# Branch merges, held modulation rounds and up products of a two-block kernel on one core

## The chip, the core and the metric

The kernel runs on one core of a Trainium2 chip. Times are device microseconds (us) of one execution. Engines: PE is TensorE (matrix products), PEld its weight load, DVE VectorE, ACT ScalarE, POOL GpSimd (here it mostly issues DMAs), SP the queue that issues the weight loads.

## The reference, cut to what is computed

256 tokens of width 1024 pass through two blocks of two layers each. All is fp32. The first block is attention with a dense feed-forward layer, then attention with a mixture of experts (MoE). The change touches the second block most:

```python
def merge_branches(y_ml, y_ga, y_na, zg, w_branch, w_out):
    gates = jax.nn.sigmoid(zg).reshape(B, T, N_BRANCH, D_MODEL)
    ys = jnp.stack([y_ml, y_ga, y_na], axis=2)
    proj = jnp.einsum('btnc,ncd->btnd', ys, w_branch)
    return jnp.sum(gates * proj, axis=2) @ w_out

def conv_ffn(h, w_up, conv_w, conv_b, w_down):
    u = h @ w_up
    up = jnp.pad(u, ((0, 0), (1, 1), (0, 0)))
    u = up[:, :-2] * conv_w[0] + up[:, 1:-1] * conv_w[1] + up[:, 2:] * conv_w[2] + conv_b
    a, g = jnp.split(u, 2, axis=-1)
    return (a * jax.nn.silu(g)) @ w_down

# second_block, for each layer l; last = (l == 1)
mod = silu(c) @ w_mod[l] + b_mod[l]          # mod_c from c_ctx alike
sh1, sc1, ga1, sh2, sc2, ga2 = split(mod, 6)
h = modulate(rms_norm(x, g_pre_mix[l]), sh1, sc1)      # hc from the context alike
... = split(h @ w_in[l])                     # three branches, and zg: 3 x 1024 gates
o = merge_branches(y_ml, y_ga, y_na, zg, w_branch[l], w_out[l])
x = x + ga1 * rms_norm(o, g_post_mix[l])
f = conv_ffn(modulate(rms_norm(x, g_pre_ffn[l]), sh2, sc2), w_up[l], conv_w[l], conv_b[l], w_down[l])
x = x + ga2 * rms_norm(f, g_post_ffn[l])
# the 256 context tokens take the same path, in layer 0 only
```

## The kernel before

**Products.** Every fp32 product is three passes in fp32r: the activations and the weights are each cut into a high and a low part, and h·h, h·l and l·h are summed in PSUM. A raw weight tile of 128x1024 (512 KB) comes in from SP's queue, ACT casts it to `wh` (L300) and DVE subtracts to `wl` (L301). Raw tiles stand in a ring of four, `wh` and `wl` in rings of four each. `gemm` (L427, `mac` L421) is **token-major**: a block of 128 tokens stands in the array and 512 weight columns move, so the result lies with tokens on the partitions. `gemm_f` (L472) is **feature-major**: a weight block stands, and the tokens move, 256 for one path or 512 where the context (c) and the image (x) go together; the result lies with features on the partitions. PSUM has three banks "mm" for products, and single banks "tr", "y", "aT", "z0", "z1"; transposes go by a product with the identity (`tr`, L323).

**Order.** A list scheduler lays out every engine's instruction stream ahead of time; it takes the instructions by their order in the program as priority. `side_by_side` (L307) and `bind` (L315) issue a run of products of which all but the first are held behind the one before.

**Modulation.** `mod` (L1031) computes `silu(c) @ w_mod` in rounds: a generator whose every `next` issues loads of `raw<-in_w_mod` on POOL's queue (four of 512 KB for layer 0, two for layer 1) and the round's products `aT<-raw,modS` (eight and four, which the profile counts as 16 and eight), through `side_by_side`. Its 12 rounds for layer 0 are called from the first block's dense feed-forward layer (`block1_dense`, L778): from the loop over the eleven groups of `w_gu` and the one over the two groups of `w_dn`; those for layer 1 from the feed-forward layer of the second block's layer 0. `mod_end` (L1058) evacuates four rounds' sum: part goes to columns, and two of the six kinds to rows in DRAM, which `gag` (L1089) broadcasts to 128 partitions and multiplies with a gain that it broadcasts too (`F<-in_row`).

**MoE.** A first pass takes 128 tokens of each expert; the largest count is read into a register on every engine and a branch goes over the second pass.

**Merge.** In `block2_layer` (L1398), `zgate` computes the gates token-major and stores them to DRAM by POOL (512 KB a path and group). After the attention the loop over the three branches j and the two column groups g loads a gate back (`zgx<-zgx`, L1565, 512 KB, one buffer a path), runs `w_br` token-major, and `mix` multiplies and adds on DVE (L1571, L1574, L1575). Then `u` is transposed (`to_feat`) and split for `w_out`.

**Feed-forward of block 2.** `block2_ffn` (L1615): in layer 1 (image only) group 0 of `w_up` is token-major, evacuated to `tm`, transposed into "tr" (eight transposes) and run through `conv` (one ACT and two DVE instructions for 128 features, L1633, L1634, L1636); groups 1 to 10 are feature-major with 256 moving tokens and run through `conv` straight from the "mm" bank.

## Time and profile before

| | us |
|---|---|
| median of 3 runs | 2661.45 |
| lowest and highest run | 2660.32, 2662.59 |
| the profiled execution's own time | 2667.87 |
| its span in the profile | 2666.1 |

| engine | busy us | share of the span | instructions |
|---|---|---|---|
| PE | 2582.1 | 97% | 13478 |
| DVE | 1778.0 | 67% | 3168 |
| ACT | 1414.4 | 53% | 2180 |
| POOL | 115.9 | 4% | 220 |

Busy time of PE overlaps from one product to the next: a product of 512 columns is listed with about 0.40 us and the next begins 0.23 us after it. So what a stretch costs PE is read from the starts. Idle time in square brackets stands with the instruction that came after it, with the event that ended it. The granted clock is the share of TensorE's full clock that a stretch had; 0.5 is its lower level.

### The profile page before, as it was taken

What the parts mean: (1) busy time and instruction counts of PE and PEld (TensorE: products, weight loads), DVE (VectorE), ACT (ScalarE), POOL (GpSimd) and SP (SyncE); (2) the same over time, 40 slices, a digit from 0 to 9 for tenths busy, and PEclk for the clock granted to TensorE, in tenths of its full rate; (3) what the DMA queues carried; (4) which work ended last, traced back from release to release, by engine and by line L of the source; (5) the groups of instructions that cost most, each with busy time, mean ns of one, the idle gap of its engine ahead of it and who ended that gap; (6) DMA issues with size and microseconds to landing.
All of it is one profiled execution on the core that took longest, in us unless ns stands there. A gap on an engine that the chain in (4) does not pass through costs nothing. (4 is left out here: it accounts for less than half of the span.)

```text
span 2666.1 us, 36388 instructions
## 1 busy us (share of the span) xinstructions
PE 2582.1 (97%) x13478; PEld 2045.5 (77%) x13478; DVE 1778.0 (67%) x3168; ACT 1414.4 (53%) x2180; POOL 115.9 (4%) x220
## 2 busy tenths in 40 slices
PE   8999999999999999899999999999999999998998
PEld 6776776778888888688777787777777787776897
DVE  5865455777888998558665567543546767667785
ACT  6644444565777777444447624432323544664563
POOL 0000110000000000000000000000100000000000
PEclk9999999999999999899999999999999999998999
DMA  6466874454889999442123355444543232455454
GB/s 188 131 194 228 296 269 177 140 177 161 327 319 341 322 332 351 150 141 88 48 64 103 127 182 179 152 165 167 174 142 99 81 127 80 134 195 185 148 184 151
DMA packets 134906, 481.30 MB, mean 181 GB/s; under 512 B 16208, under 2 KB 16368, under 8 KB 134720
## 3 DMA queue, kind: packets, MB, share of 16 engines
q1 hardware_dynamic: 109008, 389.30, 43.0%
q0 software_dynamic: 25424, 89.47, 9.6%
q8 instruction: 109, 1.79, 0.3%
q14 instruction: 77, 0.63, 0.1%
q10 hardware_dynamic: 288, 0.11, 0.0%
HBM read 466.20 MB, written 12.62 MB: 180 GB/s over the span
## 5 line engine op out<-in xcount | busy, mean ns | idle before, releaser
L301 DVE TENSOR_TENSOR wl<-raw,wh 128x1024 fp32r<-128x1024 f32 (+1 forms) x750 | 887.3, 1205 | 245.4 <-ACT wh L300 240.1
L300 ACT CAST wh<-raw 128x1024 fp32r<-128x1024 f32 (+1 forms) x750 | 760.1, 1036 | 334.8 <-PE mm L424 282.9
L423 PE MATMUL mm<-wh,oph 128*128 128x512 f32 (+1 forms) x1248 | 498.9, 401 | 12.1 <-ACT oph L300 7.6
L424 PE MATMUL mm<-wh,opl 128*128 128x512 f32 (+1 forms) x1248 | 496.1, 399 | 4.0 <-DVE opl L301 3.7
L425 PE MATMUL mm<-wl,oph 128*128 128x512 f32 (+1 forms) x1248 | 496.0, 398 | 2.5 <-DVE wl L301 2.3
L488 PE MATMUL mm<-oph,wh 128*128 128x256 f32 (+1 forms) x1024 | 343.1, 337 | 5.4 <-ACT wh L300 2.9
L490 PE MATMUL mm<-oph,wl 128*128 128x256 f32 (+1 forms) x1024 | 341.1, 337 | 0.8 <-DVE wl L301 0.7
L489 PE MATMUL mm<-opl,wh 128*128 128x256 f32 (+1 forms) x1024 | 340.9, 336 | 0.0
L423 PEld LDWEIGHTS mm<-wh,oph 128*128 128x128 f32 x1248 | 237.5, 190 | 80.9 <-ACT oph L300 9.6
L425 PEld LDWEIGHTS mm<-wl,oph 128*128 128x128 f32 x1248 | 237.2, 190 | 68.0 <-issue 12.9
L424 PEld LDWEIGHTS mm<-wh,opl 128*128 128x128 f32 x1248 | 237.8, 191 | 63.8 <-issue 8.8
L488 PEld LDWEIGHTS mm<-oph,wh 128*128 128x128 f32 x1024 | 195.5, 191 | 39.5 <-ACT wh L300 9.3
L490 PEld LDWEIGHTS mm<-oph,wl 128*128 128x128 f32 x1024 | 194.9, 191 | 25.7 <-issue 3.4
L489 PEld LDWEIGHTS mm<-opl,wh 128*128 128x128 f32 x1024 | 195.1, 191 | 20.9 <-issue 1.5
L425 PE MATMUL mm<-wl,moeH 128*128 128x512 f32 (+1 forms) x384 | 146.6, 382 | 0.0
L424 PE MATMUL mm<-wh,moeL 128*128 128x512 f32 (+1 forms) x384 | 145.3, 378 | 0.0
L423 PE MATMUL mm<-wh,moeH 128*128 128x512 f32 (+1 forms) x384 | 145.1, 378 | 0.0
L1633 ACT ACTIVATE F<-mm,cols 128x256 f32<-128x256 f32 (+1 forms) x88 | 57.9, 660 | 102.3 <-PE mm L490 102.1
L423 PE MATMUL mm<-wh,fh 128*128 128x512 f32 x264 | 105.3, 401 | 3.5 <-DVE F L1636 3.5
L1634 DVE SCALAR_TENSOR_TENSOR F<-mm,cols,F 128x255 f32<-128x255 f32 (+1 forms) x88 | 52.8, 602 | 79.9 <-ACT F L1633 78.5
L425 PE MATMUL mm<-wl,fh 128*128 128x512 f32 x264 | 104.9, 399 | 0.0
L424 PE MATMUL mm<-wh,fl 128*128 128x512 f32 x264 | 104.1, 396 | 0.0
(590 smaller groups left out, 3756.3 us busy)
## 6 DMA issues: line engine op xcount, KB each, us to landing
raw<-in_w_in SPq DMA_DIRECT2D x200, 512.0 KB, 4.2
raw<-in_w_gue SPq DMA_DIRECT2D x176, 512.0 KB, 5.5
raw<-in_w_mod POOLq DMA_DIRECT2D x96, 512.0 KB, 7.5
raw<-in_w_up SPq DMA_DIRECT2D x88, 512.0 KB, 4.7
raw<-in_w_dne SPq DMA_DIRECT2D x80, 512.0 KB, 5.0
raw<-in_w_dn SPq DMA_DIRECT2D x66, 512.0 KB, 4.5
raw<-in_w_gu SPq DMA_DIRECT2D x44, 512.0 KB, 4.7
raw<-in_w_out SPq DMA_DIRECT2D x32, 512.0 KB, 3.9
```

Of the source, the lines that this page charges most:

```text
L300: self.nc.scalar.copy(h, src)
L301: self.nc.vector.tensor_tensor(l, src, h.bitcast(F32), op=OP.subtract)
L423: mm(ps, P.h(kc, t), h, start=first, stop=False)
L424: mm(ps, P.l(kc, t), h, start=False, stop=False)
L425: mm(ps, P.h(kc, t), l, start=False, stop=last)
L488: mm(b, hj, xh, start=kc == 0, stop=False)
L489: mm(b, hj, xl, start=False, stop=False)
L490: mm(b, lj, xh, start=False, stop=kc == last)
L1633: nc.scalar.activation(o, s, AF.Identity, scale=cw[1][:, cc:cc + 1], bias=cb[:, cc:cc + 1])
L1634: nc.vector.scalar_tensor_tensor(o[:, :, 1:256], s[:, :, 0:255], cw[0][:, cc:cc + 1], o[:, :, 1:256], op0=OP.mult, op1=OP.add)
```

## The change

- `bind` has a flag `first`, by which the first product of the run is held in program order too; `mod` uses it. In `block1_dense` a round is called in each of the groups of `w_gu` from g = 1 (before: from g = 2), and after `w_dn` 1 + g rounds are called (before: 1 + 2g). There are 12 rounds, as before.
- `mod_end` multiplies the gain into the rows before they are stored; `gag` is one broadcast.
- The register of the MoE's count is read from within the first pass.
- Layer 0: `zgate` and `w_br` are feature-major, 512 tokens moving; gates come back as 128x512 pieces (2 KB in each partition) in a ring of five; `mix` works on features, and its last result is split from SBUF. The transposes of `u` go.
- Layer 1: `w_br` stays token-major; gates come back in the same ring; the transposes of each column group stand behind that group's last branch.
- Layer 1: all eleven groups of `w_up` are token-major, as group 0 was.

```diff
-    def bind(self, run):
+    def bind(self, run, first=False):
...
-            if i:
+            if i or first:
                 self.tc.keep_in_program_order(ins)
...
-                if g > 1:
+                if g:
                     next(mod, None)
...
-                for _ in range(1 + 2 * g):
+                for _ in range(1 + g):
                     next(mod, None)
...
-            self.moe_pass(sp, st, 0)
-            rv = nc.values_load(cnt[0:1, 0:1], min_val=0, max_val=S,
-                                skip_runtime_bounds_check_because="a count of at most 256 tokens")
-            with tc.If(rv > 128):
+            rv = []
+            self.moe_pass(sp, st, 0, lambda: rv.append(nc.values_load(
+                cnt[0:1, 0:1], min_val=0, max_val=S, skip_runtime_bounds_check_because="a count of at most 256 tokens")))
+            with tc.If(rv[0] > 128):
...
-                self.side_by_side(*[p for i in range(0, len(todo), 4) for p in todo[i:i + 4][::-1]])
+                self.bind([lambda p=p: nc.tensor.matmul(*p[:3], skip_group_check=True, **p[3])
+                           for i in range(0, len(todo), 4) for p in todo[i:i + 4][::-1]], first=True)
...
+                    o = ROWS[f"g_om{l}" if kind == 2 else f"g_of{l}"][0] + half * 512
+                    nc.gpsimd.dma_start(gain[p], bass.AP(tensor=src.tensor, offset=src.offset + o, ap=[[0, 2], [1, 512]]))
                     nc.vector.tensor_tensor(bias[p], bias[p], mr[p], op=OP.add)
+                    nc.vector.tensor_tensor(bias[p], bias[p], gain[p], op=OP.mult)
...
-        gp = self.f4.tile([128, D], F32, name="F4", bufs=2)
-        self.rowb(f"g_om{l}" if kind == 2 else f"g_of{l}", gp)
...
-        nc.vector.tensor_tensor(out, out, gp, op=OP.mult)
...
+                def gate(i, t):
+                    gt = sg.tile([128, 512], F32, name="zg", bufs=5)
+                    nc.gpsimd.dma_start(gt, zd[i][:, t])
+                    return gt
...
                     for g in range(2):
-                        gt = {p: sg.tile([128, 2, 512], F32, name=f"zg{p}") for p in paths}
-                        for p in paths:
-                            nc.gpsimd.dma_start(gt[p].rearrange("p a b -> p (a b)"), zd[p, 2 * j + g])
...
+                        gts = [gate(2 * j + g, t) for t in range(4 // (3 - ns))]
+                        if last:
...
+                            self.gemm("w_br", 3 * l + j, g, [("x", Pair([H[0][:, :, 0]], [L[0][:, :, 0]], 4))], epi)
+                            if j == 2:
+                                self.to_feat(u, range(4 * g, 4 * g + 4), None, lambda kc, ps: self.split(
+                                    self.XP.H[kc // 4][:, kc % 4], self.XP.L[kc // 4][:, kc % 4], ps))
+                            continue
+
+                        def epi(i0, n, c, ps, g=g, j=j, gts=gts):
+                            kc = 4 * g + c
+                            mix(j, u[:, kc], gts[c], ps)
+                            if j == 2:
+                                self.split(*(a[kc // 4][:, kc % 4].rearrange("p a b -> p (a b)")
+                                             for a in (self.opH, self.opL)), u[:, kc])
+                        self.gemm_f("w_br", 3 * l + j, g, epi, ops=(H, L))
...
-                    if last and g == 0:
...
+                    if last:
+                        def turn(tm, k):
...
+                        def epi(p, ps, k=k):
+                            tm = new()
+                            for t in range(2):
+                                self.copy(tm[:, t], ps(t))
+                            turn(tm, k)
                         self.gemm("w_up", l, g, sets, epi)
                         continue
```

Three places in the engines' streams. The first is PE in the first block's `w_gu`, where the modulation's first round stands (`aT<-raw,modS`; `oph` and `opl` are the activations' parts, `tr<-consts,s` a transpose of the group before). Before:

```order
L425 MATMUL mm<-wl,oph_96 128x512
L423 MATMUL mm<-wh,oph_96 128x512
L424 MATMUL mm<-wh,opl_98 128x512
L311 MATMUL aT<-raw,modS 32x512 x4
L425 MATMUL mm<-wl,oph_96 128x512
L423 MATMUL mm<-wh,oph_96 128x512
L424 MATMUL mm<-wh,opl_98 128x512
```

After:

```order
L423 MATMUL mm<-wh,oph_96 128x512
L424 MATMUL mm<-wh,opl_98 128x512
L325 MATMUL tr<-consts,s_2164 128x128 x2
L1057 MATMUL aT<-raw,modS 32x512 x8
L425 MATMUL mm<-wl,oph_96 128x512
L423 MATMUL mm<-wh,oph_97 128x512
L424 MATMUL mm<-wh,opl_99 128x512
```

The first half of the round's products stood in the middle of the products of one group (the second half 11 rows on); the round now stands whole, 97 rows later, behind a group's transposes. In the stream after, the rounds of layer 0 stand 44 to 63 rows apart up to `w_dn`, but for one that stands 40 rows behind the round ahead of it.

The second is POOL at the merge of layer 1, which issues the gates' DMAs (`zgx<-zgx_...` before, `zg<-zg_...` after, are the loads; `<-tm` the stores; `gax` and `gfx` the broadcast rows of `gag`). Before:

```order
L1431 DMA zgx_25022<-tm 128x1024
L1565 DMA zgx<-zgx_23628 128x1024
L1431 DMA zgx_25101<-tm 128x1024
L1565 DMA zgx<-zgx_24785 128x1024
L1565 DMA zgx<-zgx_24864 128x1024
L1096 DMA gax<-mrow_20882 128x1024
L1565 DMA zgx<-zgx_24943 128x1024
L1565 DMA zgx<-zgx_25022 128x1024
L1565 DMA zgx<-zgx_25101 128x1024
L284 DMA F_25437<-in_row 128x1024
```

After:

```order
L1435 DMA zg_24977<-tm 128x1024
L1571 DMA zg<-zg_23583 128x512 x2
L1571 DMA zg<-zg_24740 128x512 x2
L1571 DMA zg<-zg_24819 128x512
L1435 DMA zg_25056<-tm 128x1024
L1571 DMA zg<-zg_24819 128x512
L1571 DMA zg<-zg_24898 128x512 x2
L1571 DMA zg<-zg_24977 128x512
L1100 DMA gax<-mrow_20836 128x1024
L1571 DMA zg<-zg_24977 128x512
L1571 DMA zg<-zg_25056 128x512 x2
```

Six loads of 512 KB into one buffer became twelve of 256 KB into five.

The third is DVE in layer 1's `w_up` (`F<-...,cols,F` are `conv`'s two instructions, `wl` the weights' low parts, `s<-s,F` the product with the silu, `fl` the low part for `w_dn`). Before, about one group:

```order
L1634 SCALAR_TENSOR_TENSOR F_25953<-mm,cols,F_25953 128x255 x2
L1636 SCALAR_TENSOR_TENSOR F_25953<-mm,cols,F_25953 128x255 x2
L301 TENSOR_TENSOR wl<-raw,wh 128x1024
L1675 TENSOR_TENSOR s_25985<-s_25985,F_25953 128x256
L301 TENSOR_TENSOR wl<-raw,wh 128x1024
L301 TENSOR_TENSOR fl<-s_25985,fh 128x256
L301 TENSOR_TENSOR wl<-raw,wh 128x1024
L1634 SCALAR_TENSOR_TENSOR F_26039<-mm,cols,F_26039 128x255 x2
L1636 SCALAR_TENSOR_TENSOR F_26039<-mm,cols,F_26039 128x255 x2
L1675 TENSOR_TENSOR s_26071<-s_26071,F_26039 128x256
```

After, one group:

```order
L1664 SCALAR_TENSOR_TENSOR F_25881<-tr,cols,F_25881 128x255
L1666 SCALAR_TENSOR_TENSOR F_25881<-tr,cols,F_25881 128x255
L1664 SCALAR_TENSOR_TENSOR F_25881<-tr,cols,F_25881 128x255
L1666 SCALAR_TENSOR_TENSOR F_25881<-tr,cols,F_25881 128x255
L301 TENSOR_TENSOR wl<-raw,wh 128x1024
L1664 SCALAR_TENSOR_TENSOR F_25881<-tr,cols,F_25881 128x255
L301 TENSOR_TENSOR wl<-raw,wh 128x1024
L1666 SCALAR_TENSOR_TENSOR F_25881<-tr,cols,F_25881 128x255
L301 TENSOR_TENSOR wl<-raw,wh 128x1024
L295 COPY tm<-mm 128x512
L1687 TENSOR_TENSOR s_25904<-s_25904,F_25881 128x512
L301 TENSOR_TENSOR wl<-raw,wh 128x1024
```

`conv` reads "tr" instead of "mm", the copy `tm<-mm` has come in, and the products with silu are one of 512 instead of two of 256.

## Rows read from the trace of the kernel before

**Rows 1.** Page, part 1: engine, busy us, share of the span, instructions.

```profile
PE 2582.1 (97%) x13478; PEld 2045.5 (77%) x13478; DVE 1778.0 (67%) x3168; ACT 1414.4 (53%) x2180; POOL 115.9 (4%) x220
```

**Rows 2.** Waits of PE: engine, line, releaser: us in total, times, longest us.

```profile
PE aT L311 <- DMA raw<-in_w_mod: 8.5, 2, 4.4
PE z L325 <- DVE r_x L347: 8.3, 1, 8.3
```

**Rows 3.** Timeline of PE at the first rounds: start, us, instruction [idle before <-releaser].

```profile
217.79 0.39 PE L424 MATMUL mm<-wh,opl 128*128 128x512 f32 x1
222.35 1.08 PE L311 MATMUL aT<-raw,modS 128*32 128x512 f32 x4 [4.17 <-DMA raw<-in_w_mod]
...
438.43 0.40 PE L423 MATMUL mm<-wh,oph 128*128 128x512 f32 x1
443.18 1.39 PE L311 MATMUL aT<-raw,modS 128*32 128x512 f32 x8 [4.35 <-DMA raw<-in_w_mod]
```

**Rows 4.** Windows: stretch, busy us (instructions) by engine, granted clock, DMA share, GB/s.

```profile
214.00:226.00 12.00, 7.20 (x30) 3.51 (x29) 7.96 (x20) 7.80 (x14) 2.23 (x5) 0.86 1.00 400
433.00:460.00 27.00, 22.65 (x113) 14.90 (x112) 13.80 (x34) 9.78 (x17) 3.13 (x6) 0.94 0.57 200
```

**Rows 5.** Timelines of POOL and PE in a steady stretch of the rounds.

```profile
298.13 2.08 POOL L1050 DMA_DIRECT2D raw<-in_w_mod  x4 [11.60 <-PE aT L311]
...
296.77 1.92 PE L311 MATMUL aT<-raw,modS 128*32 128x512 f32 x16
310.91 1.92 PE L311 MATMUL aT<-raw,modS 128*32 128x512 f32 x16
```

**Rows 6.** Tile in_w_mod, 212 to 312 us: its DMAs' time to landing.

```profile
DMA to landing us min/median/max: 5.5/8.3/12.7
```

**Rows 7.** Timeline of PE where layer 1's rounds stood, layer 0's feed-forward layer.

```profile
1661.40 1.06 PE L311 MATMUL aT<-raw,modS 128*32 128x512 f32 x8
1664.12 0.63 PE L325 MATMUL z<-consts,tm 128*128 128x128 f32 x4 [1.65 <-DVE rs_b L351]
...
1679.18 1.07 PE L311 MATMUL aT<-raw,modS 128*32 128x512 f32 x8
1682.44 0.71 PE L488 MATMUL mm<-oph,wh 128*128 128x256 f32 x3 [2.19 <-ACT oph L300]
```

**Rows 8.** Timeline of PE at the end of layer 0's merge.

```profile
1606.90 1.03 PE L325 MATMUL z<-consts,uc 128*128 128x128 f32 x8
1608.24 0.50 PE L423 MATMUL mm<-wh,oph 128*128 128x512 f32 x1 [0.30 <-ACT oph L300]
...
1609.78 0.63 PE L325 MATMUL z<-consts,uc 128*128 128x128 f32 x4
...
1618.78 0.50 PE L423 MATMUL mm<-wh,oph 128*128 128x512 f32 x1 [1.45 <-ACT wh L300]
...
1627.12 0.50 PE L425 MATMUL mm<-wl,oph 128*128 128x512 f32 x1 [1.59 <-DVE wl L301]
```

**Rows 9.** Windows: layer 0's `w_br`, layer 1's merge, its `w_up`, ten steady groups' middle.

```profile
1539.00:1607.00 68.00, 68.00 (x293) 54.67 (x292) 42.36 (x54) 15.54 (x17) 5.83 (x11) 1.00 0.59 193
...
2378.98:2427.90 48.92, 40.07 (x162) 30.67 (x161) 30.90 (x39) 16.31 (x19) 3.71 (x7) 0.92 0.69 236
2467.58:2596.60 129.02, 126.09 (x991) 122.45 (x992) 102.94 (x170) 79.61 (x127) 0.53 (x1) 0.97 0.51 166
...
2500.00:2578.00 78.00, 78.00 (x648) 77.16 (x648) 66.39 (x109) 50.00 (x81) 0.00 (x0) 1.00 0.53 175
```

**Rows 10.** Timelines of DVE, POOL and PE in layer 1's merge.

```profile
2394.36 1.28 DVE L1571 TENSOR_TENSOR ux<-zgx,mm 128x512 f32<-128x512 f32 x2 [7.18 <-DMA zgx<-zgx]
...
2386.34 0.53 POOL L1565 DMA_DIRECT2D zgx<-zgx  x1 [5.03 <-DVE ux L1571]
...
2395.11 0.50 PE L423 MATMUL mm<-wh,yHx 128*128 128x512 f32 x1 [1.97 <-DVE ux L1571]
...
2396.92 0.63 PE L423 MATMUL mm<-wh,yHx 128*128 128x512 f32 x1
```

**Rows 11.** DMA issues: out<-in engine op xcount, KB each, median us to landing.

```profile
zgx<-zgx POOLq DMA_DIRECT2D x12, 512.0 KB, 6.2
...
kp<-in_nab POOLq DMA_DIRECT2D x16, 256.0 KB, 3.1
```

**Rows 12.** Groups by form, steady `w_up`: busy us, mean ns of one | idle before.

```profile
L301 DVE TENSOR_TENSOR wl<-raw,wh 128x1024 fp32r<-128x1024 f32 x28 | 33.1, 1220 | 0.0
L1634 DVE SCALAR_TENSOR_TENSOR F<-mm,cols,F 128x255 f32<-128x255 f32 x27 | 13.0, 480 | 1.6 <-ACT F L1633 0.8
...
L1633 ACT ACTIVATE F<-mm,cols 128x256 f32<-128x256 f32 x26 | 14.6, 562 | 1.5 <-PE mm L490 1.4
```

**Rows 13.** The same by form, of DVE in group 0: the copy into `tm`.

```profile
L295 DVE COPY tm<-mm 128x512 f32<-128x512 f32 x1 | 0.7, 682 | 0.0
```

More of the change, by code (lines that the diff above doesn't have):

```diff
@@ L470, in gemm2, with gemm_f @@
                     tepi(key, t, g, b)
-    def gemm_f(self, kind, m, g, epi, runs=((0, 2),), order=(0, 1, 2, 3)):
+    def gemm_f(self, kind, m, g, epi, runs=((0, 2),), order=(0, 1, 2, 3), ops=None):
         mm = self.nc.tensor.matmul
@@ L927, in moe_pass @@
             acts = self.moe_up(sp, cur, p, 1)
+            if p == 1 and between:
+                between()
             if p + 1 < NE // 2:
@@ L1064, in mod_end @@
             if kind in (2, 5):
-                bias = self.wk.tile([128, 512], F32, name="s5", bufs=3)
+                bias, gain = (self.wk.tile([128, 512], F32, name="s5", bufs=3) for _ in range(2))
                 src = self.I["row"]
@@ L1577, in block2_layer, with mix @@
-                for p in paths:
-                    P = PP[p]
-                    self.to_feat(u[p], range(8), None, lambda kc, ps, P=P: self.split(
-                        P.H[kc // 4][:, kc % 4], P.L[kc // 4][:, kc % 4], ps))
-        with self.scope() as so, self.scope() as self.f4:
+                def gate(i, t):
+                    gt = sg.tile([128, 512], F32, name="zg", bufs=5)
+                    nc.gpsimd.dma_start(gt, zd[i][:, t])
+                    return gt
+                def mix(j, o, gt, ps):
+                    if j == 0:
+                        nc.vector.tensor_tensor(o, gt, ps, op=OP.mult)
+                        return
+                    tmp = self.wk.tile([128, 512], F32, name="s5", bufs=3)
+                    nc.vector.tensor_tensor(tmp, gt, ps, op=OP.mult)
+                    nc.vector.tensor_tensor(o, o, tmp, op=OP.add)
@@ new lines, in block2_layer, with epi @@
+                if last:
+                    u = [sg.tile([128, D], F32, name=f"u{t}") for t in range(2)]
+                else:
+                    u = sg.tile([128, 8, 512], F32, name="u")
+                ns = len(paths)
+                for j, br in enumerate(("ml", "ga", "na")):
+                    H, L = ([sg.tile([128, 4, ns, 256], F32R, name=f"y{a}", bufs=2)] for a in "HL")
+                    for i, p in enumerate(paths):
+                        self.split(H[0][:, :, i], L[0][:, :, i], Y[br, p])
+                    for g in range(2):
+                        gts = [gate(2 * j + g, t) for t in range(4 // (3 - ns))]
+                        if last:
+                            def epi(p, ps, g=g, j=j, gts=gts):
+                                for t in range(2):
+                                    mix(j, u[t][:, g * 512:(g + 1) * 512], gts[t], ps(t))
+                            self.gemm("w_br", 3 * l + j, g, [("x", Pair([H[0][:, :, 0]], [L[0][:, :, 0]], 4))], epi)
[10 more added lines that the diff above has]
+                        self.gemm_f("w_br", 3 * l + j, g, epi, ops=(H, L))
@@ L1643, in block2_ffn @@
                     k = 2 * (g - g0)
-                    if last and g == 0:
-                        def epi(p, ps, g=g, k=k):
-                            tm = self.wk.tile([128, 2, 512], F32, name="tm", bufs=2)
-                            for t in range(2):
-                                self.copy(tm[:, t], ps(t))
+                    if last:
+                        def turn(tm, k):
                             cv = self.f4.tile([128, 4, 256], F32, name="F4", bufs=2)
@@ L1662, in epi @@
                             self.split(H[:, k:k + 2, 0], L[:, k:k + 2, 0], sg)
+                        new = lambda: self.wk.tile([128, 2, 512], F32, name="tm", bufs=2)
+                        def epi(p, ps, k=k):
+                            tm = new()
+                            for t in range(2):
+                                self.copy(tm[:, t], ps(t))
+                            turn(tm, k)
                         self.gemm("w_up", l, g, sets, epi)
@@ L1682, in epi @@
                                 self.XP.ready(0)
-                    runs = ((1, 1),) if last else ((0, 1), (1, 1)) if g == 0 else ((0, 2),)
+                    runs = ((0, 1), (1, 1)) if g == 0 else ((0, 2),)
                     self.gemm_f("w_up", l, g, epi, runs, order=(0, 2, 1, 3))
```

56 lines of the change are left out of this document (24 added, 32 removed).

## The prediction

> **What bounds the kernel now.** I read the page's busy times first: PE is busy for 97% of the span and DVE for 67% [rows 1], so only what PE executes, what PE waits for and the clock it is granted can move the end. Then I read PE's waits: the two largest entries are the modulation's weight loads, 8.5 us in two waits, and one wait of 8.3 us behind the MoE's branch [rows 2]. Last I went through the timelines of the stages that the diff touches, comparing the time of each stretch with what its instructions cost when PE waits for nothing. That cost comes from stretches at full clock: in layer 0's `w_br` 68.00 us hold 293 products of 512 columns, 0.233 us each; in layer 1's `w_up` 78.00 us hold 648 of 256 columns, 0.1204 us each [rows 9]. A transpose is 0.11 us: eight take 1.03 us and four 0.63 us with the same tail, so four more take 0.4 us [rows 8], rounded up.
>
> The profiled execution took 2667.87 us against a median of 2661.45, 0.24% more. The sum below is made in its microseconds against its own time; since its terms are waits and instructions that every run has, I take the difference over to the median unchanged.
>
> **Modulation rounds (A).** The first round's products stand in PE's stream before their weights have landed: PE starts a product at 217.79, the next thing at 222.35, so 4.56 - 0.23 = 4.3 us are lost; the second place is 438.43 to 443.18, 4.5 us lost [rows 3]. Each wait is followed by the lower clock: 0.86 over 12 us costs 1.7 us, 0.94 over 27 us costs 1.6 [rows 4]. Together 6.0 and 6.1 us. With the first product held in program order, the first round stands 97 rows later, some 22 us of products at 0.233, and its loads land in 5.5 to 12.7 us [rows 6]. So both waits end. At the first place I take back all 6.0. At the second, `mod_end` stands on DVE ahead of a weight's low part, with eight small multiplications more in all; I take 5.0. Against this, the rounds now come closer. A round's loads are issued when its predecessor's products have been read: products at 296.77, loads from 298.13 to 300.21 [rows 5], landing 5.5 to 12.7 us later, so a round that needs its last tile less than about 12.5 us after its predecessor began would wait. Rounds were 14.14 us apart [rows 5]. Of the new distances, 44 rows are just long enough (some 12 us, a wait of 0.3), and 40 rows, of which some 37 are products, give 10.8 us, a wait of about 1.3. Sum of A: -6.0 - 5.0 + 1.6 = -9.4, range -13 (no new wait, more of the DVE wait gone) to -6 (several rounds wait).
>
> Layer 1's rounds lose a hiding place. Two of them stood ahead of waits that PE had anyway, for the statistics (1.65 us) and the split (2.19 us) [rows 7]. A round of 0.7 us (eight rows counted, 1.06 with its tail) that stands there is free. After, the first comes later, among products. So two rounds cost 0.7 us each: +1.4, from 0 to +2.
>
> **MoE's count, and the gain (B, C).** In the order of the changed kernel the register load still stands immediately ahead of the branch on ACT, DVE, POOL and SP. So PE's 8.3 us there [rows 2] stay: 0. The gain's multiplication goes from `gag` to two rows; what goes is six broadcasts of 512 KB and six DVE multiplications, none of which PE's waits name. 0, with a bound of 1 us either way if a queue on POOL moves.
>
> **Layer 0 (D, E0).** The gates and `w_br` have as many products of 512 columns feature-major as token-major (96 and 288): 0. What goes is the end: 32 transposes, 32 x 0.11 = 3.5 us, and three waits of 0.30, 1.45 and 1.59 us which the transposes' evacuation causes on ACT and DVE (split parts and weights queue behind one another) [rows 8]. Together 6.8. `u` is now split from SBUF behind each branch's last group; the last features' split comes after the last products, one multiply, one add, one cast and a subtract, of which `w_out`'s first product needs a part. But the split goes by features and the early features are long done. I leave 0.8: -6.0, range -8 to -4.
>
> **Layer 1's merge (E1).** From its first `w_br` product to the steady `w_out` it is 48.92 us [rows 9], with 144 products and 16 transposes: 33.6 + 1.8 = 35.4. So 13.5 us are lost, and the chain is plain [rows 10]: POOL reissues a gate's load only when DVE has used the one buffer (2386.34), it lands 8 us later, DVE idles 7.18 us with the PSUM banks full, and PE waits 1.97 us, then runs at the lower clock (0.63 us for a product instead of 0.40). Four such waits stand in the stretch. After, the ring holds five pieces: two and a half groups, each of 24 products or 5.6 us, so 14 us ahead of the use, against the 6.2 us of a 512 KB load [rows 11]. DVE then isn't held up: per group two multiplications and two additions of 0.69 us and two weights at 1.22 are 5.2 of 5.6 us. That is close, and the end keeps a chain of mix, transposes, split and the first `w_out` product, for which I leave 3 us. -10.5, range -13 to -8.
>
> On the pieces the trace shows no price per piece: 256 KB of another 128x512 tile land in 3.1 us, 512 KB gates in 6.2 [rows 11]. The Trainium skill speaks against the change here ("Perfetto Trace Analysis", section "DMA Optimizations", rule 1: batching 2 KB transfers into 4 or 8 KB improves throughput), while its rule 2 allows that split DMAs start sooner. By rule 1 the second rival below would come out; by the row it doesn't.
>
> **Layer 1's up products (F).** Before: 129.02 us [rows 9] = 24 products of 512 (5.6) + 8 transposes (0.9) + 960 products of 256 (115.6) + 6.9 lost around group 0, where its transposes and the feature-major groups mix. After: 504 x 0.233 = 117.4, 88 transposes 9.7, together 127.1, and a part of the low clock (0.03 of 129 us, 3.9, before; I keep half, for the start that stays): 129, no change. Per group PE goes from 96 x 0.1204 = 11.56 to 48 x 0.233 + 0.88 = 12.06; the lost start pays for it. But DVE has per group four weights (4.9), eight `conv` instructions (3.8) [rows 12], a copy of 0.68 [rows 13], and a multiplication and a split of 512, some 0.7 each by the same row: 10.8 of 12.06 us, with the one "tr" bank between PE and `conv`. I take a slip of 0.3 us in ten groups: +3, range 0 to +8 (0.8 each, two-thirds of a weight's low part).
>
> By columns, 512 cost 0.233 and twice 256 cost 0.241, so 480 products save 3.7 us and the 80 new transposes cost 8.8. The Trainium skill says that larger matmuls are the more efficient ("Perfetto Trace Analysis", section "Optimizing Tensor Performance", "Matmuls"); by that alone this term would be -3.7 and the time 2633. The trace agrees on the 3%, not on the sign.
>
> **Sum.** -9.4 + 1.4 + 0 - 6.0 - 10.5 + 3 = -21.5, so 2661.45 - 21.5 = **2640 us**. Each bound added: -13 + 0 - 8 - 13 + 0 = -34 (2627) and -6 + 2 - 4 - 8 + 8 = -8 (2653). All terms are unlikely to fall on one side, but the rivals fill the upper end.
>
> **The rivals.**
> 1. *Slower: `w_up` bound by the chain over "tr".* PE's second four transposes of a group wait for the bank, `conv` on ACT (0.56) and DVE (0.48) waits for them, and weights queue behind `conv` on DVE. If PE waits 2 us in each group, the lower clock follows as it did there [rows 10]: eight products at 0.43 instead of 0.233 from start to start, 1.6 us. 3.6 x 10 = 36 in place of +3: +11.5, 2673. It makes the kernel slower from about 3.0 us lost a group. For it: DVE at 90%. Against it: 18 and 30 products (4.2 and 7.0 us) stand between the sets of transposes, and a set's `conv` needs two ACT and four DVE instructions, 1.1 and 1.9 us, and one weight ahead of it. 0.05.
> 2. *The ring doesn't hide the gates.* If a 256 KB piece took as long as a 512 KB load, and one after the other, the seven pieces beyond the first five would take 7 x 6.2 = 43 us, and with the end E1 would be -2.5: sum -13.5, 2648. For it: the queue also carries stores and broadcast rows. Against it: the 3.1 us of the 256 KB loads [rows 11]. 0.12.
> 3. *The rounds run into their loads.* If the rounds wait 0.8 us each in the ten that now follow closely, A is -3: 2646. For it: landings up to 12.7 us [rows 6]. Against it: most new distances are as long as before. 0.13.
> 4. *The count is read early after all*, against the order: of the 8.3 us some 4 would go: 2636. 0.03.
>
> **How the numbers follow.** The forecast, with its terms within their bounds, has 0.67. A measurement of this kernel can tell about 0.2%, 5.3 us, from no change: faster is below 2656.1, slower above 2666.8. Rivals 2 to 4 are faster too. Same needs two rivals and the upper end of F together, 0.05; slower is rival 1, 0.05; faster 0.90. The range is 2627 to 2654.
>
> **What would show it.** A: no wait on raw<-in_w_mod over 1.5 us, and full clock at 214 to 226. E0: no transposes between `w_br` and `w_out`, and a gap under 1 us. E1: DVE not waiting for the gate's DMA, the stretch at 38 to 39 us. F: 129 to 137 us, with small waits on `conv` or on the weights' low parts. B: the 8.3 us unchanged. It is wrong if the clock falls in `w_up`, if the second wait on DVE only moves, or if the removed waits reappear at the next shared resource, DVE.

## The result, and the profile after

The changed kernel takes 2635.31 us in the median (2634.22 to 2635.56, four runs) against 2661.8 us (2660.32 to 2662.59, four runs) on the same chip: a ratio of 0.9894, interval 0.9875 to 0.9912. That is 26.5 us less; the forecast was 21.5 less, 2640, with a range from 2627 to 2654. The two profiled executions are further apart, 2667.87 and 2635.56 us, because the one of before was 6 us above its median; where traces are compared below, that difference is in them.

The page after, its head and part 1 (busy us, share of the span, instructions), answers to [rows 1]:

```profile
span 2633.6 us, 35539 instructions
PE 2572.1 (98%) x13046; PEld 2018.1 (77%) x13046; DVE 1778.3 (68%) x3152; ACT 1417.8 (54%) x2162; POOL 126.9 (5%) x240
```

PE is as much the bound as before. The waits of PE after (engine, line, releaser: us in total, times, longest), against [rows 2]:

```profile
PE z L325 <- DVE r_x L347: 8.1, 1, 8.1
PE mm L423 <- ACT oph L300: 6.4, 3, 2.6
...
PE mm L489 <- ACT oph L300: 3.2, 1, 3.2
PE z L325 <- DVE tm L1111: 2.7, 1, 2.7
PE z L325 <- DVE rs_b L351: 2.6, 1, 2.6
```

The entry of the modulation's loads, 8.5 us before, is gone; the branch's 8.3 us are 8.1; the gates' entries are gone too. The last three waits have grown. The first and the third of them stand at the start of layer 0's feed-forward layer and were 2.2 and 1.7 us before; the one between, for the first token half's statistics at the start of layer 1's feed-forward layer, was 0.6. The first round in the timeline of PE after, against [rows 3]:

```profile
240.44 0.39 PE L325 MATMUL tr<-consts,s 128*128 128x128 f32 x2
240.75 1.92 PE L1057 MATMUL aT<-raw,modS 128*32 128x512 f32 x16
242.60 0.51 PE L425 MATMUL mm<-wl,oph 128*128 128x512 f32 x1
```

It waits for nothing: its loads were under way 28 us earlier. In the windows after (stretch, busy us by engine, granted clock, DMA share, GB/s), the first answers to [rows 4], the others to [rows 9]: layer 1's merge, layer 1's `w_up` behind its first 24 products, one group of it.

```profile
214.00:226.00 12.00, 11.17 (x46) 7.88 (x45) 9.68 (x22) 10.21 (x16) 0.78 (x2) 1.00 1.02 407
...
2356.49:2405.00 48.51, 47.64 (x210) 37.37 (x209) 37.68 (x49) 21.55 (x29) 4.84 (x9) 1.00 0.78 263
2435.18:2564.20 129.02, 128.97 (x587) 103.89 (x588) 103.20 (x152) 84.52 (x114) 0.00 (x0) 0.99 0.52 168
2470.00:2482.06 12.06, 12.06 (x58) 9.78 (x57) 9.51 (x15) 7.14 (x11) 0.00 (x0) 1.00 0.57 186
```

In 48.5 us from the merge's start PE now executes 210 matrix instructions, at full clock, where it executed 162 in 48.9 us; 160 of them are the merge, the others `w_out`. A group of `w_up` takes the 12.06 us that were worked out, PE is busy for all of it, and DVE for 9.51, not for 10.8.

### The profile page after: what moved, and what is told of

It reads as the page before. It is cut to its first block, busy times and chain, and to the rows that moved or that the text cites. A ratio compares the mean times of both kernels' runs of the same rounds, so it can differ in the third digit from the quotient of the medians.

```text
span 2633.6 us, 35539 instructions
## 1 busy us (share of the span) xinstructions
PE 2572.1 (98%) x13046; PEld 2018.1 (77%) x13046; DVE 1778.3 (68%) x3152; ACT 1417.8 (54%) x2162; POOL 126.9 (5%) x240
## 4 chain that ended last, share of the span: by engine, by line
PE 53%; DVE 3%; ACT 1%; DMA 1%; issue 0%; SPq 0%; DVEq 0%; POOL 0%; ACTq 0%
PE mm L423 7%; PE mm L424 7%; PE mm L425 7%; PE mm L489 7%; PE mm L491 7%; PE mm L490 7%; PE z L1312 2%; PE y L1317 2%; PE tr L325 1%; PE aT L1279 1%; PE aT L1057 1%; PE z L1238 1%; PE aT L325 1%; DVE wl L301 1%; PE z L325 0%
## 5 line engine op out<-in xcount | busy, mean ns | idle before, releaser
L423 PE MATMUL mm<-wh,oph 128*128 128x512 f32 (+1 forms) x1216 | 483.2, 398 | 9.2 <-ACT oph L300 6.4
L424 PE MATMUL mm<-wh,opl 128*128 128x512 f32 (+1 forms) x1216 | 482.2, 397 | 1.0 <-DVE opl L305 0.4
L489 PE MATMUL mm<-oph,wh 128*128 128x512 f32 (+1 forms) x896 | 329.5, 369 | 4.1 <-ACT oph L300 3.2
L491 PE MATMUL mm<-oph,wl 128*128 128x512 f32 (+1 forms) x896 | 328.5, 368 | 0.1
L490 PE MATMUL mm<-opl,wh 128*128 128x512 f32 (+1 forms) x896 | 328.5, 368 | 0.0
L489 PEld LDWEIGHTS mm<-oph,wh 128*128 128x128 f32 x896 | 169.9, 190 | 48.5 <-ACT wh L300 6.8
L491 PEld LDWEIGHTS mm<-oph,wl 128*128 128x128 f32 x896 | 169.5, 190 | 36.0 <-issue 7.7
L490 PEld LDWEIGHTS mm<-opl,wh 128*128 128x128 f32 x896 | 170.0, 190 | 33.3 <-issue 6.3
L1663 ACT ACTIVATE F<-mm,cols 128x512 f32<-128x512 f32 (+1 forms) x48 | 35.5, 741 | 96.5 <-PE mm L491 96.5
L1336 ACT ACTIVATE P<-z,a_sx_m 128x512 f32<-128x512 f32 (+1 forms) x96 | 58.3, 612 | 50.4 <-DVE a_sx_m L1333 50.1
```

The costliest lines, as they stand in the source:

```text
L423: mm(ps, P.h(kc, t), h, start=first, stop=False)
L424: mm(ps, P.l(kc, t), h, start=False, stop=False)
L489: mm(b, hj, xh, start=kc == 0, stop=False)
L490: mm(b, hj, xl, start=False, stop=False)
L491: mm(b, lj, xh, start=False, stop=kc == last)
L1336: nc.scalar.activation(p[j][:, :nk], z[:, :nk], AF.Exp, bias=mx, accum_out=s)
```

## The experiments

Twelve kernels ran, in three sets; each set has its own runs of before (medians 2663.76, 2663.15 and 2661.69 us). Microseconds below are the ratio's distance from 1, times the median of before.

### One part at a time

**The modulation rounds alone** (the flag, the call places, and `bind` in `mod`):

```diff
-                if g > 1:
+                if g:
                     next(mod, None)
...
-                for _ in range(1 + 2 * g):
+                for _ in range(1 + g):
...
+                self.bind([lambda p=p: nc.tensor.matmul(*p[:3], skip_group_check=True, **p[3])
+                           for i in range(0, len(todo), 4) for p in todo[i:i + 4][::-1]], first=True)
```

> The kernel before with the held modulation rounds alone. Theory (the two waits for the round's weights end, and no new ones come, since loads of a steady round landed 5 to 8 us after their issue in the changed kernel): 11 us at the first block's feed-forward layer, less 1.4 us for layer 1's rounds that no longer stand in front of waits: about 9.5 us faster than before, 2652. Rival (closer rounds run into their loads, as the forecast had it with 1.6 us and more): 8 us faster or less, with waits on raw<-in_w_mod of 0.3 us or more in the rounds.

Measured: 2654.97 us (2652.79 to 2663.03), ratio 0.9972 (0.9962 to 0.9982), 7.5 us faster (4.8 to 10.1). At the first block the theory holds: in the stretch from 200 to 470 us PE waits 0.8 us in all, for weights, and the same row of the second attention layer comes at 488.20 us where it came at 499.62, 11.4 us earlier (the starts differ by less than 0.1). No round there waits. Further on some of it is lost again, at layer 1's rounds. A new wait stands in this kernel's timeline of PE at the second of them, in the changed kernel's it is 0.25 us:

```profile
1682.68 1.07 PE L1054 MATMUL aT<-raw,modS 128*32 128x512 f32 x8 [1.15 <-DMA raw<-in_w_mod]
```

**The gain alone** (multiplied into the stored rows; `gag` without `F<-in_row`):

```diff
+                    nc.vector.tensor_tensor(bias[p], bias[p], gain[p], op=OP.mult)
...
-        self.rowb(f"g_om{l}" if kind == 2 else f"g_of{l}", gp)
...
-        nc.vector.tensor_tensor(out, out, gp, op=OP.mult)
```

> The kernel before with the gain multiplied into the stored rows, nothing else. Theory (the wait of 3.5 us in front of layer 0's last w_dn, at 2042.67 us in the trace of before, is a DVE multiplication that waits for the broadcast gain while the last convolution stands behind it on DVE): this wait and the low clock after it go, 3.5 to 5.5 us faster, 2656 to 2658. Rival (the forecast: a multiplication off PE's path, 0; the wait of before was of that one execution): within 1 us of before.

Measured: 2657.35 us (2654.77 to 2661.47), ratio 0.9979 (0.9969 to 0.9989), 5.6 us faster (2.9 to 8.3). The forecast had put this edit at nothing. The kernel before shows what it cost, in the timelines of PE and of DVE at the last `w_dn` of layer 0:

```profile
2042.67 0.40 PE L425 MATMUL mm<-wl,fh 128*128 128x512 f32 x1
2046.61 0.47 PE L423 MATMUL mm<-wh,fh 128*128 128x512 f32 x1 [3.55 <-DVE F L1636]
...
2040.52 0.74 DVE L1634 SCALAR_TENSOR_TENSOR F<-mm,cols,F 128x510 f32<-128x510 f32 x1
2044.58 1.23 DVE L1097 TENSOR_TENSOR gfx<-gfx,F 128x1024 f32<-128x1024 f32 x1 [3.32 <-DMA F<-in_row]
2045.72 0.74 DVE L1636 SCALAR_TENSOR_TENSOR F<-mm,cols,F 128x510 f32<-128x510 f32 x1
```

PE waits for a convolution; the convolution waited for nothing itself, but it stood on DVE behind the gain's multiplication, and that for a broadcast of 512 KB. After the wait the clock falls: from 2043 to 2052 the granted clock was 0.81. With the edit alone, the same two convolution instructions follow each other on DVE:

```profile
2033.40 0.74 DVE L1633 SCALAR_TENSOR_TENSOR F<-mm,cols,F 128x510 f32<-128x510 f32 x1
2034.18 0.75 DVE L1635 SCALAR_TENSOR_TENSOR F<-mm,cols,F 128x510 f32<-128x510 f32 x1
```

It was not that one execution's. PE loses 3.7 us at this place in the kernel before, and the six other kernels below and above that keep the old `gag` lose 1.1 to 3.9 us there (1.1 with the rounds held at the old call places, 2.4 or more in the other five); no kernel with the new `gag` has a wait there. The theory holds.

The old `gag` cost PE at a second place, which the theory didn't name: the wait of 1.59 us in [rows 8]. The low part that ended it stood on DVE behind the multiplication for the context's row, and that behind a broadcast:

```profile
1624.71 1.23 DVE L1097 TENSOR_TENSOR gac<-gac,F 128x1024 f32<-128x1024 f32 x1 [2.12 <-DMA gac<-mrow]
1625.85 1.22 DVE L301 TENSOR_TENSOR wl<-raw,wh 128x1024 fp32r<-128x1024 f32 x1
```

With the gain's edit alone, and layer 0's transposes still there, the low parts follow each other on DVE and PE has no such wait:

```profile
1618.28 3.48 DVE L301 TENSOR_TENSOR wl<-raw,wh 128x1024 fp32r<-128x1024 f32 x3
```

**Layer 0's merge alone** (the new branch of `zgate` and of the merge under `if not last`, the old ones under `if last`):

```diff
+                zd[i] = self.dr.tile([128, 4, 512], F32, name=f"zg{i}")
...
+                self.gemm_f("w_in2", l, 9 + i, epi)
...
+                        self.gemm_f("w_br", 3 * l + j, g, epi, ops=(H, L))
```

> The kernel before with layer 0's gates and merge feature-major, layer 1's merge as before. Theory (32 transposes at 0.11 us and the three waits behind them go): 6.0 to 7.0 us faster, 2655. Rival (the split of the last features and the weights' parts on DVE and ACT put new waits ahead of w_out): 3 us faster or less, with waits on the activations' parts at w_out's start.

Measured: 2656.7 us (2654.28 to 2660.08), ratio 0.9976 (0.9967 to 0.9985), 6.4 us faster (4.0 to 8.8). In this kernel's trace no wait of 0.6 us or more stands between the end of layer 0's `w_br` and its feed-forward layer. The changed kernel has one short wait there where [rows 8] had 0.30, 1.45 and 1.59:

```profile
1598.92 0.50 PE L423 MATMUL mm<-wh,oph 128*128 128x512 f32 x1 [0.39 <-ACT wh L300]
```

**Layer 1's merge alone** (the ring of five and the transposes by column group under `if last`, layer 0 as before):

```diff
+                    def gate(i, t):
+                        gt = sg.tile([128, 512], F32, name="zg", bufs=5)
...
+                                if j == 2:
+                                    self.to_feat(u, range(4 * g, 4 * g + 4), None, lambda kc, ps: self.split(
```

> The kernel before with layer 1's merge by the ring of five pieces and the transposes by column group, all else as before. Theory (DVE no longer waits for the gates' loads): 9 to 10.5 us faster, 2652. Rival (pieces of 256 KB in rows of 2 KB cost as much as whole loads, or the broadcast row in POOL's queue holds them): 2.5 us faster, with DVE waiting for zg<-zg as before.

Measured: 2654.94 us (2652.08 to 2656.37), ratio 0.9966 (0.9956 to 0.9977), 9.1 us faster (6.1 to 11.7). The waits that are left in its merge, on PE, 2379 to 2430 us, against 1.97 to 3.48 before:

```profile
2415.26 0.30 PE L325 MATMUL z<-consts,u 128*128 128x128 f32 x1 [0.26 <-DVE opl L301]
2417.83 0.87 PE L325 MATMUL z<-consts,u 128*128 128x128 f32 x6 [0.29 <-DVE u L1605]
2420.21 0.50 PE L423 MATMUL mm<-wh,oph 128*128 128x512 f32 x1 [0.18 <-ACT wh L300]
```

Some 2 us come back a stage later. PE's wait for the first token half's statistics, ahead of layer 1's `w_up`, in the kernel before and then in this one:

```profile
2451.48 1.09 PE L325 MATMUL z<-consts,tm 128*128 128x128 f32 x8 [0.64 <-DVE tm L1108]
```

```profile
2441.87 1.38 PE L325 MATMUL z<-consts,tm 128*128 128x128 f32 x8 [2.70 <-DVE tm L1109]
```

The changed kernel has this wait with 2.72 us.

**The up products alone:**

```diff
-                    if last and g == 0:
+                    if last:
```

> The kernel before with all of layer 1's w_up token-major, nothing else. Theory (PE alone sets the group: 48 products at 0.233 and eight transposes at 0.11, 12.06 against 11.56 us, times ten, paid for by the start's waits that go): from -1 to +1 us. Rival of the forecast (DVE, 10.8 of 12.06 us by the sum of its durations, slips 0.3 us in each group): +3 us, with PE waits on conv or weights' low parts in every group. Rival of the changed kernel's other waits (the gain comes from a better overlap that only shows together with the merge): faster by 2 us or more only in company.

Measured: 2665.56 us (2660.06 to 2670.59), ratio 1.0004 (0.9995 to 1.0014): no difference. In its trace PE waits 0.6 us in all from 2465 to 2600. The five parts alone sum to 7.5 + 5.6 + 6.4 + 9.1 - 1.1 = 27.5 us; together they gave 28.2 by the ratio and 26.5 by the medians. So the parts add within the intervals. The wait of 1.59 us is in two of them: it ended with the gain's edit alone and with layer 0's merge alone.

### What in each part did it

**The rounds held, but called where they were:**

```diff
+                self.bind([lambda p=p: nc.tensor.matmul(*p[:3], skip_group_check=True, **p[3])
+                           for i in range(0, len(todo), 4) for p in todo[i:i + 4][::-1]], first=True)
```

> The kernel before with the rounds' first product held, rounds called where before called them (from the third group of w_gu, 1 + 2g after w_dn). Theory (holding alone ends both waits; the earlier calls only spread the rounds): the same as with both, 2655 on the scale of the runs of before at 2663.8, within 1 us. Rival (the call places do it: with three rounds after the second w_dn group, two of them run without products between): 3 to 5 us less gained, as a wait for raw<-in_w_mod at the end of w_dn.

Measured: 2662.24 us (2659.37 to 2671.76), ratio 1.0000 (0.9990 to 1.0011): nothing is gained, where 2655 was expected. The theory that holding ends both waits falls. The first wait is gone, the second isn't. PE's timeline:

```profile
432.47 0.39 PE L423 MATMUL mm<-wh,oph 128*128 128x512 f32 x1
438.06 1.94 PE L1054 MATMUL aT<-raw,modS 128*32 128x512 f32 x8 [5.19 <-DMA raw<-in_w_mod]
```

With three rounds called after `w_dn`'s second group, one finds no products in front of it to cover its loads, held or not. Calling them one group earlier, and two at the end, is what ends this wait. The first wait's end is worth something in this trace: the row of the second attention layer that came at 499.62 us comes at 494.68, 4.9 us earlier. That nothing of it is left at the end points to a price of holding further on, and the next kernel looks for it at layer 1's rounds:

**The changed kernel with only layer 0's rounds held:**

```diff
-                           for i in range(0, len(todo), 4) for p in todo[i:i + 4][::-1]], first=True)
+                           for i in range(0, len(todo), 4) for p in todo[i:i + 4][::-1]], first=l == 0)
```

> The changed kernel, but layer 1's modulation rounds are not held: the scheduler may put their first product early again, as before, where two rounds stood in front of waits for statistics. Theory: 1 to 2 us faster than the changed kernel, 2633.5 to 2634.5 where that has 2635.3, with rounds in front of the waits at layer 0's feed-forward start. Rival (a round there delays the products behind it as much as it hides): no difference.

Measured: 2630.97 us (2630.27 to 2631.84), ratio 0.9877 (0.9860 to 0.9893). The changed kernel's runs were 2634.22 to 2635.56, in another set; the ranges don't meet, the medians are 4.3 us apart, and the intervals of the two ratios overlap. The two kernels with other rings below, which hold layer 1's rounds too, ran in 2633.41 to 2638.79 us. It is the fastest kernel of this study. The rounds stand in front of the waits again, as in [rows 7]. PE's timeline in this kernel:

```profile
1641.05 1.07 PE L1057 MATMUL aT<-raw,modS 128*32 128x512 f32 x8
1643.76 0.63 PE L325 MATMUL z<-consts,tm 128*128 128x128 f32 x4 [1.65 <-DVE rs_b L351]
...
1657.44 1.07 PE L1057 MATMUL aT<-raw,modS 128*32 128x512 f32 x8
1660.69 0.62 PE L489 MATMUL mm<-oph,wh 128*128 128x256 f32 x3 [2.19 <-ACT oph L300]
```

and at the same place of the changed kernel:

```profile
1642.34 0.63 PE L325 MATMUL z<-consts,tm 128*128 128x128 f32 x4 [2.64 <-DVE rs_b L351]
...
1660.72 1.01 PE L489 MATMUL mm<-oph,wh 128*128 128x256 f32 x3 [3.18 <-ACT oph L300]
```

The windows of 25 us around it, first the changed kernel, then the one with layer 0's rounds held only:

```profile
1639.00:1664.00 25.00, 19.13 (x134) 18.43 (x133) 18.52 (x59) 16.25 (x35) 2.10 (x4) 0.86 0.40 139
```

```profile
1640.00:1665.00 25.00, 21.02 (x171) 18.33 (x169) 18.74 (x59) 16.69 (x36) 4.46 (x8) 1.00 0.62 226
```

The gap is the same either way; with a round in it, PE is idle for 1 us less in each, and this execution kept the full clock. From a wait in layer 0's early projections (1141.36 us in the changed kernel) to the last wait ahead of layer 1 (2069.24), the traces are 5.3 us apart (922.6 against 927.9 us). Two rounds of 0.7 us are 1.4 of that, the loads' wait 0.4, and 0.14 x 25 = 3.5 us are the clock. The stretch from DVE's first `tm<-X,r_oxb` to its first `tm<-C,r_gcb`, which holds these waits and rounds, takes 395.9 to 398.3 us in the four traces that have the new `gag` and late rounds (behind the waits), and 392.3 to 394.0 in the three that have the new `gag` and early rounds (in front of them). The clock part is not as certain as the rest: behind these two waits the lower clock came 7 times of 16 in the eight traces with early rounds (idle for 1.65 and 2.19 us) and 10 times of 12 in the six with late ones (2.64 and 3.18 us). In the kernel before it came both times.

**Layer 1's ring alone, transposes at the end** (the kernel with layer 1's merge alone, but):

```diff
-                            if j == 2:
-                                self.to_feat(u, range(4 * g, 4 * g + 4), None, lambda kc, ps: self.split(
+                            if j == 2 and g:
+                                self.to_feat(u, range(8), None, lambda kc, ps: self.split(
```

> Like the kernel with layer 1's merge alone changed, but all 16 transposes stand behind the last branch, as before; only the gates' ring of five 256 KB pieces is new. Theory (the wait for the one gate buffer is the whole loss): 7 to 8 us of that kernel's 9 remain, the rest at the end (transposes bunched, a wait on the activations' low part of 2 us). Rival (the interleaved transposes carry the gain): 4 us or less.

Measured: 2654.73 us (2650.97 to 2659.97), ratio 0.9964 (0.9951 to 0.9977), 9.6 us faster: as much as with the interleaved transposes. I had expected 1 to 2 us less. The ring carries the gain; the place of the transposes shows no difference.

**Two pieces in layer 1's ring in place of five:**

```diff
-                    gt = sg.tile([128, 512], F32, name="zg", bufs=5)
+                    gt = sg.tile([128, 512], F32, name="zg", bufs=2 if last else 5)
```

> The changed kernel with two gate pieces of 256 KB in layer 1's ring instead of five (layer 0 keeps five). Theory (the depth ahead of the use is what counts): the buffers of one group, as before, so the waits of DVE for the gates come back: 6 to 9 us slower than the changed kernel, 2641 to 2644. Rival (loads in halves start sooner and land in about 3 us, so that two suffice): under 2 us slower.

Measured: 2635.42 us (2633.73 to 2638.79), ratio 0.9901 (0.9884 to 0.9918). The theory falls: two pieces are as good as five, with the bytes of the one buffer of before. DVE does wait for gates, four times (timeline of DVE in this kernel's merge), and PE has one wait that the changed kernel hasn't:

```profile
2364.34 0.69 DVE L1576 TENSOR_TENSOR u<-zg,mm 128x512 f32<-128x512 f32 x1 [2.04 <-DMA zg<-zg]
2367.03 0.69 DVE L1576 TENSOR_TENSOR u<-zg,mm 128x512 f32<-128x512 f32 x1 [0.86 <-DMA zg<-zg]
2376.10 0.69 DVE L1579 TENSOR_TENSOR s<-zg,mm 128x512 f32<-128x512 f32 x1 [1.32 <-DMA zg<-zg]
2384.49 0.69 DVE L1579 TENSOR_TENSOR s<-zg,mm 128x512 f32<-128x512 f32 x1 [1.05 <-DMA zg<-zg]
...
2386.97 0.88 PE L325 MATMUL z<-consts,u 128*128 128x128 f32 x6 [0.91 <-DVE u L1580]
```

The last row is PE's. With halves, the first half is reloaded while the second is still in use, and a half lands in 4.2 us in the median where the whole took 6.2 [rows 11]; so DVE's waits fall from 7.18 and 4.13 us to 2.04 and less, and no product of `w_br` waits for them. I read that as the slack of the "mm" banks; a run that takes a bank away was not made.

**Whole loads in two buffers** (512 KB a group, rows of 4 KB):

```diff
+                        if last:
+                            gw = sg.tile([128, 2, 512], F32, name="zgw", bufs=2)
+                            nc.gpsimd.dma_start(gw, zd[2 * j + g])
+                            gts = [gw[:, t] for t in range(2)]
```

> The changed kernel with layer 1's gates loaded as 512 KB a group into two buffers (rows of 4 KB), in the place of five pieces of 256 KB. Theory (depth, not size): one group ahead of use, 5.6 us at PE's pace, against loads of 4 to 6 us, so it just holds: within 1 us of the changed kernel. Rival (pieces of 2 KB rows cost more than whole loads): faster by 1 us or more. Rival (landings of 6 to 8 us under the weights' traffic): 2 to 4 us slower, with waits of DVE on the gate.

Measured: 2634.52 us (2633.41 to 2637.13), ratio 0.9893 (0.9877 to 0.9908): no difference to the pieces. DVE waits 0.6 us once. So neither depth five nor the size of the pieces matters here; what the single buffer lacked was that a load could start before the last use.

### How far the up products are from DVE's bound

Each group's two copies into `tm` on DVE, three times over, in the changed kernel:

```diff
-                                self.copy(tm[:, t], ps(t))
+                                for _ in range(3):
+                                    nc.vector.tensor_copy(tm[:, t], ps(t))
```

> The changed kernel with more work for DVE in layer 1's w_up: each of a group's two copies into tm is done on DVE and three times over (before one on ACT, one on DVE), some 5 x 0.6 = 3.0 us a group more. In the changed kernel DVE is busy 9.5 of 12.06 us a group. Theory (DVE decides only once its work exceeds PE's): 12.5 a group, so 0.5 to 1 us a group, 5 to 11 us slower. Rival (the chain over the one tr bank decides, since the copies stand ahead of the transposes): 2 us a group and the low clock after each wait, over 25 us slower.

Measured: 2647.72 us (2644.98 to 2650.33), ratio 0.9946 (0.9932 to 0.9960), 12.4 us slower than the changed kernel by the medians. Nearly four groups of `w_up`, in a window of this kernel (columns as above):

```profile
2507.00:2555.00 48.00, 46.43 (x211) 36.77 (x212) 46.32 (x71) 26.91 (x37) 0.00 (x0) 1.00 0.56 174
```

DVE is now busy for 46.32 of 48.00 us, and PE waits. From the start of the second token half of its first group to its last product the stage took 135.4 us, 7.5 more than in the changed kernel; most of the rest is a wait of 2.55 us at the start of `w_dn` with the low clock behind it. The sign and the first term are the theory's, the end was not in it. The chain over the one "tr" bank, which was to cost over 25 us, doesn't decide: PE's waits for transposes in the whole stage are 0.3 us.

### A version that was to be faster yet

With only layer 0's rounds held, and twelve products of `w_up`'s second group moved in front of the second token half's statistics:

```diff
+                    P.ready(0)
+                    b = self.acc()
+                    part(b, 0, w0)
+                    self.copy(tu[0][:, 0], b)
+                    b1 = self.acc()
+                    part(b1, 0, w1)
+                    P.ready(1)
```

> The changed kernel with layer 1's modulation rounds not held, and besides the first two groups of layer 1's w_up begun together: twelve products of the second group's first token half stand ahead of the second half's statistics, 36 products to cover them instead of 24. Theory (2.8 us more of cover where PE waits 0.9 and 2.1 us and then has the low clock): 3 to 4 us faster than without it, 2627 to 2628. Rival (the second group's weights take DVE and ACT from the statistics' chain, or fx as the place of tm delays the end): no gain or slower.

Measured: 2635.71 us (2631.59 to 2637.19), ratio 0.9896 (0.9879 to 0.9914): no gain over the changed kernel, and 4.7 us behind the kernel without the twelve products, in another set. The rival is right. The first wait of the stage, for the first half's statistics, in this kernel and then in the one without:

```profile
2419.69 1.97 PE L325 MATMUL z<-consts,tm 128*128 128x128 f32 x8 [5.56 <-DVE r_oxa L347]
```

```profile
2414.34 1.97 PE L325 MATMUL z<-consts,tm 128*128 128x128 f32 x8 [2.71 <-DVE tm L1111]
```

The 2.8 us that the cover was to bring are lost one step earlier, where the wait is 2.85 us longer; and the wait that the twelve products were to cover, for the second half's activations, is still 2.09 us (0.72 and 1.82 without them). DVE's timeline bears the rival out: the statistics end there at 2412.73 us and the sum that uses them begins at 2415.07, because a weight's low part stands between, which waited 1.20 us for its cast on ACT; without the twelve products the sum begins 0.04 us behind the statistics. So ACT's cast and DVE's low part both have a share; no run separates them.

## Why the prediction was right, and where it wasn't

| term | forecast | alone, measured (interval) |
|---|---|---|
| A, layer 1's rounds included | -9.4 + 1.4 = -8.0 | -7.5 (-10.1 to -4.8) |
| C, the gain | 0 | -5.6 (-8.3 to -2.9) |
| E0, layer 0's merge | -6.0 | -6.4 (-8.8 to -4.0) |
| E1, layer 1's merge | -10.5 | -9.1 (-11.7 to -6.1) |
| F, up products | +3 | +1.1 (-1.3 to +3.7) |
| sum | -21.5 | -27.5; all together -26.5 by the medians |

**A** came out nearly as a sum, but by luck, from two errors. The new waits that I charged, 1.6 us, didn't come: I took the longest landing of [rows 6], 12.7 us, for a round's last load, but that belongs to the first loads. In the changed kernel a steady round's loads landed 5 to 9 us after their issue (one round's last 11.0), and from 220 to 420 us the median is 7.2, so 40 rows of distance are enough. The trace has 11.4 us gained by the second layer's attention where the forecast had 9.4. Against that, the term for layer 1's rounds was too small: +1.4, from 0 to +2. The medians with and without holding them are 4.3 us apart and the traces 5.3. I had counted what the rounds cost elsewhere, 1.4, and had left out a wait of their loads and the clock behind a longer idle stretch, though the first part of A had charged just that at the other two places. The mechanism of the prediction, holding, was half of the matter: without the new call places the second wait stays, and the 4.9 us that holding gave at the first are about what it costs at layer 1's rounds. No run holds layer 0's rounds alone at the old call places, so this split is read from the traces.

**C** is the step that failed in kind. "Six DVE multiplications, none of which PE's waits name" looked at releasers only. The wait of 3.55 us was in the list of waits, under the convolution that released it; the multiplication stood one place ahead of that on DVE. The releaser of a wait is the last instruction of a queue, and what was late may be the one before it. The second place was even in the prediction's rows, the wait of 1.59 us, booked under the transposes.

**E0** was right in size. Of its three waits the one of 1.59 us came from the gain's multiplication and not from the transposes, though this edit alone ended it too. **E1** was right in size and in naming DVE's wait for the single buffer, wrong in what removes it: five pieces and 14 us of lead aren't needed, two pieces or two whole buffers do as well. Of the 3 us left for the end the merge itself loses 1.3: from 2356.02 to 2395.44 us, 39.4 us, it and `w_out`'s first twelve products hold 156 products and 16 transposes, 38.1 by the prediction's costs. Another 2.1 come back at the statistics ahead of `w_up`, a wait on DVE that the prediction didn't look at, though it named DVE as the place where removed waits could reappear. The gates' pieces landed in 4.5 us in the median, not in the 3.1 of the other tile in [rows 11]; that was still early enough. The row on landings decided against rule 1 of the Trainium skill ("Perfetto Trace Analysis", section "DMA Optimizations", given there for kernels bound by DMA, while PE is busy for 98% of this one); the runs agree with the row, since pieces in 2 KB rows and whole loads in 4 KB rows differ by 0.9 us, inside the spread. Its rule 2, that split DMAs let some start sooner, is what the kernel with two pieces shows.

**F**: PE's side was exact, 12.06 us a group. The slip of 0.3 us a group didn't come. DVE's 10.8 us were a sum of listed durations, and those overlap: the window shows 9.51. The slack is 2.5 us a group, and 3 us of added copies used it up. Rival 1 makes the kernel slower from 3.0 us lost in each group; even with the added copies it was 7.5 us in the whole stage.

**B and D** went as said: the 8.3 us stay at 8.1, and `w_br`'s 288 products in layer 0 take 67.2 us feature-major where they took 67.0.

Rivals: none of the four came true in the changed kernel. The mechanism of one could be produced, rounds that run into their loads by calling three at the end. With added work DVE bounds `w_up` too, but not through the chain of rival 1.

## What to carry to other kernels

Before an operation off the bounding engine is costed at nothing, look on its own engine at what stands directly behind it, and whether PE waits for that. Take DVE's load from the busy time of a window, not from a sum of durations. When a wait is removed, look one stage on at the next wait for the same engine. Where PE must idle for a statistic, independent work that fills the gap is worth more than its own length if a longer gap brings the lower clock.

## What the runs showed of the hardware

Waits of DVE for its operands of up to 2 us held up no product of `w_br` in the merge with two pieces, while waits of 4 to 7 us cost 2 to 3 us each in the kernel before. The lower clock (0.5 of the full one) did not come each time behind the same idle stretch of PE: behind the two waits at layer 0's feed-forward layer it came 7 times of 16 where PE idled 1.65 and 2.19 us, and 10 times of 12 where it idled 2.64 and 3.18 us. Listed durations on DVE overlap: 10.8 us by their sum were 9.51 us of a window.
